# Five seven-product quads in each pass of the attention branch, with U summed ahead for four of them

## The chip, the cores and the metric

The kernel runs on one NeuronCore of a Trainium2 chip. The core has engines with queues of their own: TensorE (PE: matmuls and transposes, PEld: its weight loads), VectorE (DVE), ScalarE (ACT), GpSimd (POOL) and SyncE (SP, which issues most DMAs). Each engine works through its own list strictly in order, and waits where the next instruction needs something that another engine or a transfer has not yet delivered. The metric is the device time of one execution in microseconds.

## The reference

One layer of a hybrid block on 256 tokens of width 2048, in float32: a normed input is projected to q, k, v, gates and the inputs of a state-space part; attention with dilated windows over 16 heads and the state-space part each give a branch, which are merged through gates and projected once more.

```
hn = rms_norm(x, norm_w)
proj = hn @ w_in                                   # q, k, v, z_a, z_s, xbc, dt, g_a, g_s
...
o_a = o_a.reshape(b, s, ATTN_WIDTH) * jax.nn.silu(z_a)
...
merged = jax.nn.sigmoid(g_a) * (o_a @ w_attn_branch) + jax.nn.sigmoid(g_s) * (y @ w_ssm_branch)
return x + merged @ w_out
```

The change concerns the product `o_a @ w_attn_branch` (256 x 2048 by 2048 x 2048), called the attention branch below.

## The kernel before

**Splitting.** A float32 product is made of three matmuls on rounded parts: each factor is split into a high part h (a rounded copy) and a low part l (the rest), and `triple` adds xh·h, xh·l and xl·h. Weights come in units of 128 x 1024 (512 KB each), loaded by SyncE (L267) into a ring of five. For each unit ScalarE writes h (L278) and VectorE l = w - h (L279).

**Stages.** The units follow one another through the whole program: the state-space part until 744 us, v to 828, then 16 heads of q, k and za (828 to 1116), the gate ga (1116 to about 1200), the attention branch (about 1197 to 1284) and the output projection (to 1369). The last three, and v, go through `gemm_pair`.

**gemm_pair** makes 256 rows by 1024 columns in one pass, so that each stage has pass 0 (columns 0 to 1023) and pass 2 (1024 to 2047). It goes through eight quads; a quad is two rows of blocks of the weight (2 x 128 of the inner dimension). A plain quad takes two units and 24 matmuls of 128x512. A quad named in `S_QUADS` takes its 2 x 2 blocks by seven products (the Strassen-Winograd form), 21 matmuls. For it one needs sums of weights: A (wa, one whole unit, L530), C (wc, half a unit, L534), T (wt, 1024 wide, L533) and U = A's unit less T2, the right half of T. It also needs sums on the left, `sx_o`, made once for each quad from the heads' results (`keep_left`), kept in DRAM and fetched again (`fetch_left`, on POOL's queue). Each of A, C, T and U is split by ScalarE (L551) and VectorE (L552). The products that are shared go to four accumulators pp, the others straight to ps. `close`: the last quad of a pass, a plain one, finishes ps block by block.

**Sums ahead.** T of every such quad of ga, attn and out is made earlier: `sum_jobs` hangs, behind certain weight units of the heads, a load of two pieces (`get`), and three units later two subtracts and a transfer to DRAM (`add`, `spill`). There are 21 such jobs, one every 15/4 units. U is made in the branch itself: L565 on VectorE, between the splits of C and T.

**The end of a pass.** When all quads of seven products are in, `fold` (L589 to L594) adds the four accumulators pp together, L1154 adds ps, and `merge` (L1143, L1144) multiplies by the gate and adds the other branch: sixteen VectorE operations of 128x512, which give th_s. `turn_m` (L1136) transposes th_s on TensorE into banks "g", and `split` (L286, L288) writes mT, the left factor of the output projection. The accumulators pp of pass 2 lie in the same banks "g". `A_ORDERS` sets the order of the quads in each pass of the branch. The program's order decides the order on each engine, except where `high_priority` pulls a part forward (the splits of a quad, and the fold and merge of pass 2).

Of the kernel before, what the change touches and what calls it, by code (L numbers as in the profile page):

```python
# [15 lines left out]
P = 128  # L16
# [24 lines left out]
A_ORDERS = {0: (0, 1, 2, 4, 3, 6, 5, 7), 2: (0, 2, 1, 4, 3, 5, 6, 7)}  # L41
# [11 lines left out]
    ("attn", 0): (2, 4, 6), ("attn", 2): (2, 4, 5, 6), ("out", 0): (3, 5), ("out", 2): (3, 5),  # L53
# [6 lines left out]
O_BEHIND = 3, 14, 15, 17  # L60
SUMS_ATT = [(t, q) for t in [(n, c) for n in ("ga", "attn", "out") for c in (0, 2)] for q in S_QUADS[t]]
ATT_QUADS = sorted({*S_QUADS[("attn", 0)], *S_QUADS[("attn", 2)]})
# [136 lines left out]
def hybrid_block(ctx: ExitStack, tc: tile.TileContext, wall, xt, x, pk_d, cst_d, fw_d, out):  # L199
# [31 lines left out]
    presum, lefts = {}, {}  # L231
    ssm_pool = []

    def behind_unit(n, f):
        on_unit.setdefault(n, []).append(f)
# [8 lines left out]
    def sum_jobs(jobs, units, places):  # L244

        def get(tag, q, t, b11, behind):
            n = FIRST[tag] + 2 * q
            for dst, src in ((t, wall[n + 1]), (b11, wall[n, :, :512])):
                gp.tensor_copy(dst[:, 0:1], behind)
                nc.sync.dma_start(dst, src)  # L250

        def add(tag, q, t, b11, res, behind):
            gp.tensor_copy(res[:, 0:1], behind)
            ve.tensor_tensor(res[:, :512], t[:, :512], b11, ALU.subtract)
            ve.tensor_tensor(res[:, 512:], t[:, 512:], res[:, :512], ALU.subtract)
            spill(presum, (tag, q), f"t_{tag[0]}{tag[1]}_{q}", res, [UNIT])

        for n, ((tag, q), u) in enumerate(zip(jobs, units)):
            t, b11, res = places[n % len(places)]
            behind_unit(u, lambda behind, a=(tag, q, t, b11): get(*a, behind))  # L260
            behind_unit(u + SUM_LAG, lambda behind, a=(tag, q, t, b11, res): add(*a, behind))
# [207 lines left out]
    def gemm_pair(tag, x_of, n_kt, sxs, swap, extra={}, close=1, order=None, room={}, tail=None):  # L469
# [22 lines left out]
        for at, q in enumerate(order):  # L492
# [57 lines left out]
            def part(src, h, l):  # L550
                ac.activation(h, src, AF.Copy)  # L551
                ve.tensor_tensor(l, src, h.bitcast(F32), ALU.subtract)  # L552

            two = lambda t: t.rearrange("p (k m) -> p k m", k=2)
            with tc.high_priority(L_AHEAD):
# [8 lines left out]
                t2 = wt[:, 512:].unsqueeze(1).to_broadcast([P, 2, 512])  # L564
                ve.tensor_tensor(two(wa), two(wa), t2, ALU.subtract)  # L565
# [3 lines left out]
                part(wa, hu, lu)  # L569
# [122 lines left out]
    with tc.tile_pool(name="ssm", bufs=2) as sp:  # L692
# [212 lines left out]
        for c in GS_BEFORE[0]:  # L905
# [7 lines left out]
            [(sums_at[:, 0], sums_at[:, 2, :512], sums_at[:, 1])],  # L913
# [130 lines left out]
    with tc.tile_pool(name="att", bufs=2) as ap:  # L1044
# [33 lines left out]
        def mix(h, pT, za):  # L1078
# [10 lines left out]
            if h % 2 == 1 and q in ATT_QUADS:  # L1089
# [37 lines left out]
    with tc.tile_pool(name="fin", bufs=2) as fp:  # L1127
        fin = big.tile([P, 2, D], F32, name="fin", tag="yo1a")
        room = {"wt": [fin[:, i, UNIT:] for i in range(2)], "wc": [fin[:, i, :512] for i in range(2)]}
# [31 lines left out]
        attend(2)  # L1161
        for n in range(4):
            after(M_LAG + 1 + n // 2, lambda a=(2 + n // 2, n % 2, ("m1", "m2")[n % 2]): turn_m(*a))
# [119 lines left out]
```

## Time and profile before

| what | before |
|---|---|
| median of 3 runs | 1379.91 us (1379.5 to 1380.3) |
| the profiled execution | 1379.87 us, its span 1378.0 us |
| TensorE busy | 1366.8 us, granted clock 0.998 of full speed |
| VectorE busy | 1177.0 us |
| ScalarE busy | 840.0 us |
| heads, 828 to 1116 us | VectorE 218.31 of 288, DMA share 0.83 |
| attention branch, 1200 to 1284 us | TensorE 84.00, VectorE 75.21, DMA share 0.66 |

The span runs from the first to the last instruction that the profiler saw; the execution's own time has 1.87 us around it. Busy time of an engine is a sum over its instructions. In the lists of waits a row reads: engine and instruction that waited, what it waited for, then the total in us, how often, and the longest. In a timeline a row reads: start, length, engine, line, operation, output<-inputs, shapes, count.

### The profile page before, as it was taken

Reading aid. Unit: us, or ns where it says so; the run is one execution under the profiler, and the core shown is the slowest. Engines: PE = TensorE matmul, PEld = TensorE weight load, DVE = VectorE, ACT = ScalarE, POOL = GpSimd, SP = SyncE. Lnnn points to the kernel's source line nnn. Section 1 sums busy time; section 2 is a strip of 40 time slices with the busy share of each in tenths; the row PEclk is TensorE's granted clock in tenths of the full one; section 3 lists DMA queues with packets and bytes.
Section 4 is the critical chain, followed back from the end, with each engine's and each line's share of the span. In section 5 each row is a group of like instructions: output and inputs, shape, how many; then the busy total and the mean of one; then the engine's idle time right before and its main releaser. Section 6 shows DMA issues by size and latency. Waiting matters only on the chain.

```text
span 1378.0 us, 20734 instructions
## 1 busy us (share of the span) xinstructions
PE 1366.8 (99%) x7260; PEld 1164.8 (85%) x7260; DVE 1177.0 (85%) x1763; ACT 840.0 (61%) x1310; POOL 161.7 (12%) x238
## 2 busy tenths in 40 slices
PE   9999999999999999999999999999999999999997
PEld 7888888888888888888888888888888888888886
DVE  6898899898899888788989888777877789988897
ACT  7655777675667676666565554454444557655564
POOL 2301211101020100010001001211211000400112
PEclk9999999999999999999999999999999999999999
DMA  9767878778787867578677568888889757875773
GB/s 342 237 190 237 298 267 286 262 244 288 248 277 237 298 203 220 174 242 277 228 261 270 211 215 316 306 275 280 306 298 302 230 163 267 291 244 173 246 273 122
DMA packets 106520, 348.15 MB, mean 253 GB/s; under 512 B 11888, under 2 KB 14256, under 8 KB 106416
## 3 DMA queue, kind: packets, MB, share of 16 engines
q1 hardware_dynamic: 104400, 340.67, 74.0%
q10 hardware_dynamic: 1440, 4.06, 0.8%
q0 software_dynamic: 576, 2.10, 0.4%
q8 instruction: 57, 0.93, 0.3%
q14 instruction: 47, 0.39, 0.1%
HBM read 316.97 MB, written 29.82 MB: 252 GB/s over the span
## 4 chain that ended last, share of the span: by engine, by line
PE 98%; DMA 0%; DVE 0%; ACT 0%; issue 0%; SPq 0%; POOL 0%; POOLq 0%; DVEq 0%
PE ps_xs L333 8%; PE ps_zs L333 8%; PE ps_k L333 4%; PE ps_za L333 4%; PE ps_q L333 4%; PE ps_zs L339 4%; PE ps_xs L339 4%; PE ps_ssm L485 3%; PE ps_ssm L486 3%; PE ps_ssm L484 3%; PE ps_q L339 2%; PE ps_za L339 2%; PE ps_k L339 2%; PE ps_gs L421 2%; PE ps_gs L422 2%; PE ps_gs L420 2%
## 5 line engine op out<-in xcount | busy, mean ns | idle before, releaser
L278 ACT ACTIVATE h<-w 128x1024 fp32r<-128x1024 f32 (+1 forms) x394 | 410.0, 1048 | 306.0 <-issue 73.7
L279 DVE TENSOR_TENSOR l<-w,h 128x1024 fp32r<-128x1024 f32 (+1 forms) x394 | 474.0, 1209 | 111.1 <-ACT h L278 106.9
L333 PE MATMUL ps_zs<-XT,h 128*128 128x512 f32 x496 | 172.0, 393 | 0.0
L333 PE MATMUL ps_xs<-XT,h 128*128 128x512 f32 x496 | 171.6, 393 | 0.0
L339 PE MATMUL ps_zs<-XT,l 128*128 128x256 f32 x496 | 134.6, 279 | 0.0
L339 PE MATMUL ps_xs<-XT,l 128*128 128x256 f32 x496 | 133.7, 277 | 0.0
L333 PEld LDWEIGHTS ps_xs<-XT,h 128*128 128x128 f32 x496 | 91.3, 188 | 19.4
L333 PEld LDWEIGHTS ps_zs<-XT,h 128*128 128x128 f32 x496 | 91.3, 188 | 18.9
L339 PEld LDWEIGHTS ps_zs<-XT,l 128*128 128x128 f32 x496 | 93.3, 188 | 2.1
L339 PEld LDWEIGHTS ps_xs<-XT,l 128*128 128x128 f32 x496 | 93.2, 188 | 2.1
L333 PE MATMUL ps_q<-XT,h 128*128 128x512 f32 x256 | 91.1, 404 | 0.0
L333 PE MATMUL ps_k<-XT,h 128*128 128x512 f32 x256 | 88.6, 395 | 0.0
L333 PE MATMUL ps_za<-XT,h 128*128 128x512 f32 x256 | 88.4, 394 | 0.0
L551 ACT ACTIVATE ha<-wa 128x1024 fp32r<-128x1024 f32 x45 | 47.5, 1056 | 45.9 <-PE ps_ssm L486 10.0
L339 PE MATMUL ps_q<-XT,l 128*128 128x256 f32 x256 | 68.4, 278 | 0.0
L339 PE MATMUL ps_k<-XT,l 128*128 128x256 f32 x256 | 68.4, 277 | 0.0
L339 PE MATMUL ps_za<-XT,l 128*128 128x256 f32 x256 | 68.4, 277 | 0.0
L552 DVE TENSOR_TENSOR la<-wa,ha 128x1024 fp32r<-128x1024 f32 x45 | 54.8, 1218 | 8.4 <-ACT ha L551 8.3
L552 DVE TENSOR_TENSOR ltu<-wa,htu 128x1024 fp32r<-128x1024 f32 x40 | 48.7, 1219 | 10.8 <-ACT htu L551 10.8
L793 ACT ACTIVATE gt<-acb,acT 128x128 f32<-128x128 f32 x128 | 44.1, 390 | 22.2 <-DMA acb<-acum_d 21.9
L333 PEld LDWEIGHTS ps_k<-XT,h 128*128 128x128 f32 x256 | 47.0, 188 | 9.9
L333 PEld LDWEIGHTS ps_q<-XT,h 128*128 128x128 f32 x256 | 47.1, 188 | 9.7
(691 smaller groups left out, 3347.8 us busy)
## 6 DMA issues: line engine op xcount, KB each, us to landing
w<-in_wall SPq DMA_DIRECT2D x390, 512.0 KB, 4.8
wa<-in_wall SPq DMA_DIRECT2D x45, 512.0 KB, 4.7
th_a<-in_wall SPq DMA_DIRECT2D x21, 512.0 KB, 4.7
sums_at<-in_wall SPq DMA_DIRECT2D x18, 512.0 KB, 5.0
acb<-acum_d SPq DMA_DIRECT2D x32, 256.0 KB, 3.8
t_ssm<-sums_at SPq DMA_DIRECT2D x13, 512.0 KB, 4.3
wt<-t_ssm SPq DMA_DIRECT2D x13, 512.0 KB, 4.7
th_a<-in_wall SPq DMA_DIRECT2D x21, 256.0 KB, 5.4
```

Of the source, the lines that this page charges most:

```text
L278: ac.activation(h[:, a:b], w[:, a:b], AF.Copy)
L279: ve.tensor_tensor(l[:, a:b], w[:, a:b], h[:, a:b].bitcast(F32), ALU.subtract)
L333: high = pe.matmul(acc, h[:, kk, :], xs_of(kt), start=(kt == 0), stop=False)
L339: low = pe.matmul(acc[:, S:], l[:, kk, :], xs_of(kt)[:, :S], start=False, stop=(kt == KT - 1))
L420: pe.matmul(accs[i], xh, h[:, kk], start=(kt == 0), stop=False)
L421: pe.matmul(accs[i], xh, l[:, kk], start=False, stop=False)
L484: pe.matmul(acc, xh, h, start=start, stop=False)
L485: pe.matmul(acc, xh, l, start=False, stop=False)
L486: pe.matmul(acc, xl, h, start=False, stop=stop)
L551: ac.activation(h, src, AF.Copy)
L552: ve.tensor_tensor(l, src, h.bitcast(F32), ALU.subtract)
L793: ac.activation(g4[:, n, b], acb[:, j, b // 2 * P : b // 2 * P + P], AF.Relu, scale=-1.0, bias=sc[:, h : h + 1],)
```

## The change

In both passes of the branch the quads 2 to 6 use seven products (before: 2, 4, 6 in pass 0, and 2, 4, 5, 6 in pass 2), in the order 0, 2, 3, 1, 4, 5, 6, 7. For quads 3 to 6 U is summed ahead with T: the job then loads the whole second unit, makes one more subtract of 1024 and one more transfer to DRAM; the branch loads U (wu, L550 of the changed kernel) and leaves the subtract out. The 24 jobs come every 17/5 units. Their result lies in the pool of the converted units ("lt") and no longer in th_a. wu and wc lie in a pool of their own, `room_a`. A fifth left factor, for quad 3, is fetched together with the first.

```diff
-A_ORDERS = {0: (0, 1, 2, 4, 3, 6, 5, 7), 2: (0, 2, 1, 4, 3, 5, 6, 7)}
+A_ORDERS = {0: (0, 2, 3, 1, 4, 5, 6, 7), 2: (0, 2, 3, 1, 4, 5, 6, 7)}
...
-    ("attn", 0): (2, 4, 6), ("attn", 2): (2, 4, 5, 6), ("out", 0): (3, 5), ("out", 2): (3, 5),
+    ("attn", 0): (2, 3, 4, 5, 6), ("attn", 2): (2, 3, 4, 5, 6), ("out", 0): (3, 5), ("out", 2): (3, 5),
...
-O_BEHIND = 3, 14, 15, 17
+U_QUADS = 3, 4, 5, 6
+O_BEHIND = 3, 3, 14, 15, 17
...
+SUMS_U = {(t, q) for t, q in SUMS_ATT if t[0] == "attn" and q in U_QUADS}
...
-        def get(tag, q, t, b11, behind):
+        def get(tag, q, t, b, behind):
             n = FIRST[tag] + 2 * q
-            for dst, src in ((t, wall[n + 1]), (b11, wall[n, :, :512])):
+            b = b if (tag, q) in SUMS_U else b[:, :512]
+            for dst, src in ((t, wall[n + 1]), (b, wall[n, :, : b.shape[-1]])):
                 gp.tensor_copy(dst[:, 0:1], behind)
                 nc.sync.dma_start(dst, src)
 
-        def add(tag, q, t, b11, res, behind):
+        def add(tag, q, t, b, res, behind):
+            res = res(f"t_{tag[0]}{tag[1]}_{q}")
             gp.tensor_copy(res[:, 0:1], behind)
-            ve.tensor_tensor(res[:, :512], t[:, :512], b11, ALU.subtract)
+            ve.tensor_tensor(res[:, :512], t[:, :512], b[:, :512], ALU.subtract)
             ve.tensor_tensor(res[:, 512:], t[:, 512:], res[:, :512], ALU.subtract)
             spill(presum, (tag, q), f"t_{tag[0]}{tag[1]}_{q}", res, [UNIT])
+            if (tag, q) in SUMS_U:
+                t2 = res[:, 512:].unsqueeze(1).to_broadcast([P, 2, 512])
+                two = b.rearrange("p (k m) -> p k m", k=2)
+                ve.tensor_tensor(two, two, t2, ALU.subtract)
+                spill(u_sums, (tag, q), f"u_{tag[0]}{tag[1]}_{q}", b, [UNIT])
...
+            if (tag, q) in u_sums:
+                wu = place("wu")
+                nc.sync.dma_start(wu, u_sums[tag, q])
...
-                t2 = wt[:, 512:].unsqueeze(1).to_broadcast([P, 2, 512])
-                ve.tensor_tensor(two(wa), two(wa), t2, ALU.subtract)
+                if (tag, q) not in u_sums:
+                    wu = wa
+                    t2 = wt[:, 512:].unsqueeze(1).to_broadcast([P, 2, 512])
+                    ve.tensor_tensor(two(wa), two(wa), t2, ALU.subtract)
                 ht, lt = pair_of("t")
                 part(wt, ht, lt)
                 hu, lu = pair_of("u")
-                part(wa, hu, lu)
+                part(wu, hu, lu)
...
-            SUMS_ATT, [FIRST[("q", 0)] + 3 + n * 15 // 4 for n in range(len(SUMS_ATT))],
-            [
-                (th_a[:, i, :UNIT], th_a[:, 1, UNIT + 512 * i : UNIT + 512 * i + 512], th_a[:, 0, UNIT:])
-                for i in range(2)
-            ],
+            SUMS_ATT, [FIRST[("q", 0)] + 3 + n * 17 // 5 for n in range(len(SUMS_ATT))],
+            [(th_a[:, i, :UNIT], th_a[:, i, UNIT:]) for i in range(2)],
+            lambda name: mul.tile([P, UNIT], F32, name=name, tag="lt", bufs=2),
...
-    with tc.tile_pool(name="fin", bufs=2) as fp:
+    with tc.tile_pool(name="branch", bufs=1) as bp:
         fin = big.tile([P, 2, D], F32, name="fin", tag="yo1a")
-        room = {"wt": [fin[:, i, UNIT:] for i in range(2)], "wc": [fin[:, i, :512] for i in range(2)]}
+        spots = bp.tile([P, 3 * UNIT], F32, name="room_a", tag="room_a")
+        room = {
+            "wt": [fin[:, i, UNIT:] for i in range(2)],
+            "wu": [spots[:, i * UNIT : (i + 1) * UNIT] for i in range(2)],
+            "wc": [spots[:, 2 * UNIT + i * 512 : 2 * UNIT + i * 512 + 512] for i in range(2)],
+        }
```

What stands where on the engines, at three places of the program. In the names, `attn0` and `attn2` are the passes; the first number after h, l, ha, la, hc, lc, htt, ltt, htu, ltu is the weight unit (pass 0 has 417 to 432, pass 2 has 433 to 448, two for each quad, so that 429 is quad 6 of pass 0 and 437 quad 2 of pass 2), and the last number only tells buffers apart.

VectorE, from the first fold operation of pass 0 on (the sum of pp_attn0_2). Before:

```order
L591 TENSOR_TENSOR fin_12298<-pp_attn0_2_12380,fin_12298 128x512
L279 TENSOR_TENSOR l432_12589<-w432_12586,h432_12588 128x1024
L552 TENSOR_TENSOR ltt437_12721<-fin_12298,htt437_12720 128x1024
L592 TENSOR_TENSOR fin_12298<-pp_attn0_3_12381,fin_12298 128x512
L593 TENSOR_TENSOR fin_12298<-fin_12298 128x512
L279 TENSOR_TENSOR l433_12670<-w433_12667,h433_12669 128x1024
L594 TENSOR_TENSOR fin_12298<-fin_12298 128x512
L279 TENSOR_TENSOR l434_12676<-w434_12673,h434_12675 128x1024
L1154 TENSOR_TENSOR fin_12298<-ps_attn0_0_12299,fin_12298 128x512
L1154 TENSOR_TENSOR fin_12298<-ps_attn0_1_12300,fin_12298 128x512
L1143 SCALAR_TENSOR_TENSOR th_a_7802<-th_a_7802,fin_12298 128x512 x2
L1154 TENSOR_TENSOR fin_12298<-ps_attn0_2_12301,fin_12298 128x512
```

And in the changed kernel:

```order
L605 TENSOR_TENSOR fin_12386<-pp_attn0_2_12433,fin_12386 128x512
L606 TENSOR_TENSOR fin_12386<-pp_attn0_3_12434,fin_12386 128x512
L1171 TENSOR_TENSOR fin_12386<-ps_attn0_0_12388,fin_12386 128x512
L564 TENSOR_TENSOR ltt437_12822<-fin_12386,htt437_12821 128x1024
L607 TENSOR_TENSOR fin_12386<-fin_12386 128x512
L1160 SCALAR_TENSOR_TENSOR th_a_7802<-th_a_7802,fin_12386 128x512
L564 TENSOR_TENSOR la437_12813<-wa437_12808,ha437_12812 128x1024
L564 TENSOR_TENSOR lc437_12817<-room_a_12387,hc437_12816 128x512
L608 TENSOR_TENSOR fin_12386<-fin_12386 128x512
L1171 TENSOR_TENSOR fin_12386<-ps_attn0_1_12389,fin_12386 128x512
L1161 SCALAR_TENSOR_TENSOR th_s_90<-th_a_7802,th_s_90 128x512
L579 TENSOR_TENSOR wa437_12808<-wa437_12808,fin_12386 128x1024
```

What moved: the splits of quad 7 (l432) and of the first quad of pass 2 (l433, l434) stood among the fold, and now stand ahead of it; the splits of quad 2 of pass 2 (la437, lc437, U437) stand among it instead. The list goes on with:

```order
L564 TENSOR_TENSOR la439_12856<-wa439_12850,ha439_12855 128x1024
L1171 TENSOR_TENSOR fin_12386<-ps_attn0_2_12390,fin_12386 128x512
L1171 TENSOR_TENSOR fin_12386<-ps_attn0_3_12391,fin_12386 128x512
L564 TENSOR_TENSOR lc439_12860<-room_a_12387,hc439_12859 128x512
L1160 SCALAR_TENSOR_TENSOR th_a_7802<-th_a_7802,fin_12386 128x512
L288 TENSOR_TENSOR l435_12895<-w435_12892,h435_12894 128x1024
L564 TENSOR_TENSOR ltu437_12826<-wa437_12808,htu437_12825 128x1024
L1160 SCALAR_TENSOR_TENSOR th_a_7802<-th_a_7802,fin_12386 128x512 x2
L1161 SCALAR_TENSOR_TENSOR th_s_90<-th_a_7802,th_s_90 128x512
L288 TENSOR_TENSOR l436_12901<-w436_12898,h436_12900 128x1024
```

TensorE, from the last matmul on pp_attn0_2 on. Before:

```order
L486 MATMUL pp_attn0_2_12380<-htt429_12515,sx_o6_12315 128x512
L484 MATMUL ps_attn0_0_12299<-h427_12546,oaTb_10585 128x512
L484 MATMUL ps_attn0_1_12300<-h427_12546,oaTb_10585 128x512
L484 MATMUL ps_attn0_3_12302<-h427_12546,oaTb_10585 128x512
L484 MATMUL pp_attn0_3_12381<-htu429_12519,sx_o6_12315 128x512
L484 MATMUL ps_attn0_2_12301<-htu429_12519,oaTb_10585 128x512
L485 MATMUL ps_attn0_0_12299<-l427_12547,oaTb_10585 128x512
L486 MATMUL ps_attn0_0_12299<-h427_12546,oaTb_10585 128x512
L485 MATMUL ps_attn0_1_12300<-l427_12547,oaTb_10585 128x512
```

And in the changed kernel:

```order
L495 MATMUL pp_attn0_2_12433<-htt429_12652,sx_o6_12404 128x512
L494 MATMUL pp_attn0_3_12434<-ltu429_12657,sx_o6_12404 128x512
L495 MATMUL pp_attn0_3_12434<-htu429_12656,sx_o6_12404 128x512
L494 MATMUL ps_attn0_2_12390<-ltu429_12657,oaTb_10649 128x512
L495 MATMUL ps_attn0_2_12390<-htu429_12656,oaTb_10649 128x512
L493 MATMUL ps_attn0_2_12390<-h431_12683,oaTb_10649 128x512
L494 MATMUL ps_attn0_2_12390<-l431_12684,oaTb_10649 128x512
L495 MATMUL ps_attn0_2_12390<-h431_12683,oaTb_10649 128x512
L493 MATMUL ps_attn0_2_12390<-h432_12689,oaTb_10649 128x512
```

What moved: before, quad 5 (unit 427) and quad 7 stood behind the last products of quad 6; now only quad 7 does, whose first blocks (ps_attn0_0, 1 and 3) stand even ahead of them. Further on TensorE begins the quads of pass 2 and the transposes; before, around the first l of quad 1 (435):

```order
L1136 MATMUL mtp10_12653<-cst_77,th_s_90 128x128 x3
L1136 MATMUL mtp11_12660<-cst_77,th_s_90 128x128 x3
L485 MATMUL ps_attn2_1_12636<-lc437_12716,sx_o2_12082 128x512
L486 MATMUL ps_attn2_1_12636<-hc437_12715,sx_o2_12082 128x512
L484 MATMUL ps_attn2_1_12636<-h435_12751,oaTa_8484 128x512
L484 MATMUL ps_attn2_2_12637<-htu437_12724,oaTa_8484 128x512
L485 MATMUL ps_attn2_0_12635<-l435_12752,oaTa_8484 128x512
L486 MATMUL ps_attn2_0_12635<-h435_12751,oaTa_8484 128x512
```

and in the changed kernel from the place where la of quad 3 is used:

```order
L494 MATMUL ps_attn2_0_12736<-la439_12856,oaTa_8484 128x512
L495 MATMUL ps_attn2_0_12736<-ha439_12855,oaTa_8484 128x512
L493 MATMUL ps_attn2_0_12736<-h435_12894,oaTa_8484 128x512
L494 MATMUL ps_attn2_1_12737<-lc439_12860,sx_o3_12170 128x512
L495 MATMUL ps_attn2_1_12737<-hc439_12859,sx_o3_12170 128x512
L493 MATMUL ps_attn2_1_12737<-h435_12894,oaTa_8484 128x512
L494 MATMUL ps_attn2_0_12736<-l435_12895,oaTa_8484 128x512
```

What moved: quad 3 (439) with its la and lc has come in between quad 2 and quad 1, and twelve of the sixteen transposes stand behind quad 1 now. From the last matmul on pp_attn0_2 to the first on pp_attn2_0 stood 112 matmuls and 16 transposes before, and 61 and 16 in the changed kernel.

More of the change, by code (lines that the diff above doesn't have):

```diff
@@ L230, in hybrid_block @@
     on_unit = {}
-    presum, lefts = {}, {}
+    presum, u_sums, lefts = {}, {}, {}
     ssm_pool = []
@@ L912, in hybrid_block @@
             SUMS_SSM, [FIRST[("B", g)] + n for g in range(1, 7) for n in SUM_UNITS],
-            [(sums_at[:, 0], sums_at[:, 2, :512], sums_at[:, 1])],
+            [(sums_at[:, 0], sums_at[:, 2, :512])], lambda name: sums_at[:, 1],
         )
@@ L1161, in hybrid_block @@
         attend(2)
+    with tc.tile_pool(name="fin", bufs=2) as fp:
         for n in range(4):
```

8 lines of the change are left out of this document (4 added, 4 removed).

## The prediction

> **What bounds the kernel now.** I read the page from the chain of work backwards, and asked first whether the engine that the chain names ever stops.
>
> ```profile
> span 1378.0 us, 20734 instructions
> PE 1366.8 (99%) x7260; PEld 1164.8 (85%) x7260; DVE 1177.0 (85%) x1763; ACT 840.0 (61%) x1310; POOL 161.7 (12%) x238
> PE 98%; DMA 0%; DVE 0%; ACT 0%; issue 0%; SPq 0%; POOL 0%; POOLq 0%; DVEq 0%
> PE warm L630 <- DVE ssq L627: 1.4, 1, 1.4
> PE ps_first L385 <- ACT h L278: 1.4, 2, 1.1
> ```
>
> 98% of the chain is TensorE, and the two last rows are the whole answer of the view of waits for that engine: three waits, 2.8 us, in 1378 us. So the kernel is as long as its row of matmuls, and two things alone change the time: fewer matmuls, or a wait that TensorE does not have today. The price of a matmul is read where the attention branch runs:
>
> ```profile
> 1226.52 0.39 PE L484 MATMUL ps_attn<-hc,sx_o 128*128 128x512 f32 x1
> ...
> 1227.88 0.39 PE L485 MATMUL pp_attn<-ltt,sx_o 128*128 128x512 f32 x1
> ```
>
> The first column is the start. Six steps take 1.36 us: 0.227 us for each matmul, though each row lasts 0.39 (they overlap).
>
> **What goes.** A plain quad issues 24 matmuls, one with seven products 21. The branch goes from seven such quads (three, then four) to ten: 9 matmuls fewer, 9 x 0.227 = **-2.04 us**. That is all that the change can gain, since TensorE waits for nothing that could go away.
>
> **What is added in the heads (828 to 1116 us).** Three more sums (21 to 24), and eight of them now also make U.
>
> ```profile
> 828.00:1116.00 288.00, 288.00 (x1684) 253.15 (x1683) 218.31 (x417) 142.25 (x220) 43.57 (x63) 1.00 0.83 281
> L254 DVE TENSOR_TENSOR th_a<-th_a x21: 681/691/693, 836.1 to 1063.6; 128x512 f32<-128x512 f32 x21
> L565 DVE TENSOR_TENSOR wa<-wa,fin x7: 1214/1217/1218, 1208.1 to 1273.7; 128x1024 f32<-128x1024 f32 x7
> ACT h L278 <- PE ps_za L333: 31.8, 20, 1.8
> ACT h L278 <- PE ps_k L333: 18.7, 11, 1.8
> ACT h L278 <- PE ps_q L333: 13.6, 11, 1.6
> ```
>
> The columns of the first row are the length, then the busy time of PE, PEld, DVE, ACT and POOL, the granted clock, the DMA share and GB/s. VectorE has 288 - 218 = 70 us free. It gets 6 subtracts of 0.69, 8 of 1.22 and one more left factor (six small operations, estimated at 2.5 us from the 0.69 of a row 512 wide): some 16 us. The last three rows show who leads: ScalarE's conversions wait for TensorE to give buffers back (its list of waits here has no row that ends on a weight load). So the conversions run ahead, and the added subtracts take from that lead: **0 us**. If the cover were gone, each would cost at most its own 1.2 us.
>
> The loads are nearer their limit. Over seven heads (126 us, at 288 / 16 = 18 each) the order of SyncE's queue now has 45.4 MB where it had 37.2 (86.5 pieces of 512 KB, not 71: three sums more, U's other half loaded, U spilled). The row's 281 GB/s at a share of 0.83 would be 338 at a share of 1, and 45.4 MB at 338 are 134 us: 8 us late over these heads if 338 were the limit. But more has been moved elsewhere:
>
> ```profile
> 1196.00:1202.00 6.00, 6.00 (x28) 4.99 (x27) 4.65 (x7) 2.80 (x4) 0.99 (x3) 1.00 1.00 382
> ```
>
> At 382 GB/s they take 119 us, inside 126. I take 0, being nearer to a rate that was measured at full share than to a scaled one, and keep 8 us as the other end. [...]
>
> The new loads of U (512 KB each, in place of nothing) fall into 1160 to 1284:
>
> ```profile
> 1160.00:1200.00 40.00, 39.98 (x178) 32.80 (x176) 37.94 (x41) 27.73 (x34) 14.72 (x8) 1.00 0.83 283
> 1200.00:1242.00 42.00, 42.00 (x187) 34.79 (x186) 37.91 (x43) 24.84 (x29) 0.00 (x0) 1.00 0.74 250
> 1242.00:1284.00 42.00, 42.00 (x195) 34.83 (x194) 37.30 (x45) 24.07 (x31) 3.16 (x1) 1.00 0.58 184
> ```
>
> Shares of 0.83, 0.74 and 0.58 leave room for eight of them (4 MB, 11 us at 382 GB/s, beside 84 us of the branch). The two first stand in SyncE's queue ahead of the load of wa407; its first use moves some 24 matmuls (5.4 us) later in TensorE's order, more than the 2.7 us that two such loads take. **0 us.** Inside the passes a further quad of seven costs VectorE 1.5 conversions more, and U ahead saves it a subtract; counted along the order, VectorE's lead grows in pass 0 and stays above 2 us at the step to the last product.
>
> **The hand-over from pass 0 to pass 2 is what decides.** VectorE ran here in before, in the order that the change touches:
>
> ```profile
> 1229.90 0.68 DVE L591 TENSOR_TENSOR fin<-pp_attn,fin 128x512 f32<-128x512 f32 x1
> ...
> 1237.57 1.28 DVE L1154 TENSOR_TENSOR fin<-ps_attn,fin 128x512 f32<-128x512 f32 x2
> 1238.77 1.28 DVE L1143 SCALAR_TENSOR_TENSOR th_a<-th_a,fin 128x512 f32<-128x512 f32 x2
> ...
> 1247.65 2.35 DVE L279 TENSOR_TENSOR l<-w,h 128x1024 fp32r<-128x1024 f32 x2
> 1249.92 1.22 DVE L552 TENSOR_TENSOR ltu<-wa,htu 128x1024 fp32r<-128x1024 f32 x1
> 1251.06 2.47 DVE L288 TENSOR_TENSOR mT<-mtp,mT 128x512 fp32r<-128x512 f32 x4
> 1249.04 2.04 ACT L286 ACTIVATE mT<-mtp 128x512 fp32r<-128x512 f32 x4
> 1247.16 0.82 PE L1136 MATMUL mtp<-cst,th_s 128*128 128x128 f32 x6
> 1247.73 0.48 PE L484 MATMUL ps_attn<-hc,sx_o 128*128 128x512 f32 x1
> 1255.57 0.39 PE L484 MATMUL pp_attn<-ha,oaTa 128*128 128x512 f32 x1
> ```
>
> From start to start an operation 512 wide costs 1.20 / 2 = 0.60 us (1237.57 to 1238.77), one of 1024 costs 2.27 / 2 = 1.135 us (1247.65 to 1249.92), and a transpose 0.57 / 6 = 0.095 us of TensorE (1247.16 to 1247.73). The fold can begin only when the last product of pp_attn0_2 is in. Then sixteen operations of 512 (fold, add, merge) lead to th_s, its transposes, mT, and only then does pp_attn2_0 get the banks that the transposes used. In before, TensorE had 112 matmuls and 16 transposes between that last product and the first of pp_attn2_0 (25.4 + 1.5 = 26.9 us; the trace has 1228.1 to 1255.57). The sixth place in the order held the last quad of seven, with two plain quads behind it. In the new order it is the seventh with one behind it, and the rows of order leave **61 matmuls and 16 transposes**: 13.8 + 1.5, with about 0.3 for switching, 15.6 us.
>
> VectorE's list from L605 on is the sixteen, and mixed into them the conversions that pass 2 starts with. Up to l436 stand 16 operations of 512 and 7 of 1024 (ltt437, la437, U437, la439, l435, ltu437, l436): 16 x 0.60 + 7 x 1.135 + 0.3 for start and end = 17.85 us after the last product. TensorE would like l436 after 55 matmuls and 4 transposes: 12.9 us. It comes 4.95 us late; la439 (made at 10.2, wanted at 8.8), lc439 (12.0, 9.5) and l435 (13.8, 10.2) are late before it, as parts of the same wait. From l436 on stand six matmuls (1.4), twelve transposes (1.1), and ScalarE's copy and VectorE's split of the first part of mT (0.51 and 0.62, quarters of the rows of four). pp_attn2_0 would start at 20.4 if the two lay wholly beside the later transposes, at 21.5 if none of it did; I take 21.15, since only part of the transposes is left once the first bank is full. That is 21.15 instead of 15.6: **+5.55 us**.
>
> How sure is the count? The same count for before gives every tile there at least 0.7 us of lead, and TensorE indeed does not wait. Where both can be compared, the count can be kind:
>
> ```profile
> 1242.97 1.22 DVE L552 TENSOR_TENSOR la<-wa,ha 128x1024 fp32r<-128x1024 f32 x1
> ...
> 1246.61 0.48 PE L485 MATMUL ps_attn<-la,oaTa 128*128 128x512 f32 x1
> ```
>
> la437 was ready at 1244.19 and used at 1246.61, a lead of 2.4 us where the count has 4.6. So the wait is bounded by 4.1 us below (VectorE's list as far as mT alone, 19.7, against 15.6) and by 7 above (most of those 2.2 us more). I take 5.55, which the rows give as they stand.
>
> **The sum,** made against the profiled run: 1379.87 (span 1378.0 and 1.87 around it; the median is 1379.91, so they are one): 1379.87 - 2.04 + 5.55 = **1383.4 us**.
>
> **The rivals.** *The hand-over is covered*: TensorE keeps running, only the nine matmuls count: 1379.87 - 2.04 = 1377.8, on the faster side. For it speaks that TensorE waits nowhere in before, though VectorE is as full there (37.9 of 42 us). It decides where VectorE reaches l436 in 12.9 us instead of 17.85, which needs each operation at 72% of the measured price, or five of the sixteen and two conversions gone from ahead of it. Against it stands that the list is a fixed order. 0.19.
> *The loads of the heads bind*: at 338 GB/s seven heads are 8 us late, of which a ring of loads hides some; with the hand-over 1388 to 1392. For it: VectorE and SyncE issue in order, and a share of 0.83 is high. Against: 382 was reached, and before shows no wait for a load. 0.09.
> *Half the wait*: if the sums and merges that stand ahead of la439 and l435 found gaps to run in, some 2.8 us of wait would remain: 1380.6. VectorE's list has no gap there by the count, so this stays thin: 0.02.
>
> **How the numbers follow.** The forecast has 0.70, from 1382.0 to 1385.0 by its bounds of 4.1 and 7 (1381.9 and 1384.8, rounded). To leave out no more than 2 in 10 the range goes down to the covered hand-over: 1377.6 to 1385.4; what it leaves out is mostly the loads. A difference under 0.2% (2.76 us: 1377.1 to 1382.6) is about what a measurement of this kernel can't tell from no change. The lower end of the forecast lies inside that, so of its 0.70 I count 0.14 as the same and 0.56 as slower; the loads add 0.02 and 0.07. The covered hand-over is the same but for 0.03 (2.04 us are not 2.76), 0.16, and half the wait adds 0.02: faster 0.03, same 0.34, slower 0.63.
>
> **What would show it.** In the trace of after, right: 354 matmuls in the branch; TensorE's list of waits has rows on la, lc and l of L564 and L288 for VectorE between the two passes, some 4 to 7 us, and the granted clock stays at 1.00. Wrong: no such row and the end near 1377.8; or waits between 828 and 1116 us for h or l behind a weight load; or an order of the merge that leaves more than 61 matmuls ahead of pp_attn2_0.

## The result, and the profile after

| | before | changed kernel |
|---|---|---|
| median | 1380.30 us (5 runs, 1379.5 to 1381.0) | 1389.19 us (5 runs, 1388.2 to 1391.4) |
| ratio | 1 | 1.0067, interval 1.0054 to 1.0079 |
| the profiled execution | 1379.87 us, span 1378.0 | 1388.82 us, span 1387.0 |

The change costs 8.9 us, where 3.5 were forecast. Each ratio, here and below, is to runs of the kernel before that were taken beside it; their medians lie between 1380.3 and 1381.0 us, so that differences to before can be compared between experiments more safely than times. The page of the changed kernel, its span, busy times and the chain that ended last, and then the view of waits for TensorE, without its four rows of 0.2 and 0.3 us (instruction that waited, what for, total in us, times, longest):

```profile
span 1387.0 us, 20876 instructions
PE 1370.0 (99%) x7251; PEld 1164.8 (84%) x7251; DVE 1190.0 (86%) x1784; ACT 845.2 (61%) x1317; POOL 168.7 (12%) x249
PE 95%; DVE 2%; DMA 1%; issue 1%; ACT 1%; POOL 0%; SPq 0%; POOLq 0%; ACTq 0%; DVEq 0%
PE ps_out L495 <- DVE mT L297: 2.0, 1, 2.0
PE ps_attn L494 <- DVE l L288: 1.5, 2, 0.8
PE warm L644 <- DVE ssq L641: 1.4, 1, 1.4
PE ps_attn L493 <- ACT htu L563: 0.9, 1, 0.9
PE ps_first L394 <- ACT h L287: 0.8, 1, 0.8
PE ps_attn L494 <- DVE lc L564: 0.6, 1, 0.6
PE pp_attn L493 <- DVE mT L297: 0.4, 1, 0.4
PE ps_attn L493 <- ACT h L287: 0.4, 1, 0.4
...
```

Two rows of waits have become twelve, and the chain has 95% of TensorE instead of 98%. TensorE has 9 matmuls fewer (7251 for 7260) and is yet busy for 3.2 us more: some of what is lost counts as busy time, so the rows of waits do not hold it all. I went along the starts of TensorE's matmuls instead, and added up by how much each step from start to start is longer than the usual 0.227 us (0.095 for a transpose). From the gate to the end this gives four places:

| place | lost, us |
|---|---|
| gate (1149) | 0.45 |
| first hand-over, pass 0 to pass 2 (1247 to 1260.3) | 5.80 |
| end of pass 2 (1283 to 1285) | 1.02 |
| second hand-over, branch to output projection (1308 to 1314) | 3.86 |
| 9 matmuls less | -2.04 |
| sum | 9.09 (the spans differ by 9.0) |

By the same count the kernel before loses about 0.3 us at the first hand-over and 0.2 at the second, so that the sum comes within 0.1 us of the spans partly by luck.

**The first hand-over** went as the count along the lists had it. VectorE's and TensorE's timeline of the changed kernel (start, length, engine, line, operation):

```profile
1238.94 0.69 DVE L605 TENSOR_TENSOR fin<-pp_attn,fin 128x512 f32<-128x512 f32 x1 [4.21 <-PE pp_attn L495]
...
1255.57 1.21 DVE L288 TENSOR_TENSOR l<-w,h 128x1024 fp32r<-128x1024 f32 x1
...
1238.52 0.39 PE L495 MATMUL pp_attn<-htt,sx_o 128*128 128x512 f32 x1
...
1256.84 0.50 PE L494 MATMUL ps_attn<-l,oaTa 128*128 128x512 f32 x1 [0.69 <-DVE l L288]
...
1260.25 0.50 PE L493 MATMUL pp_attn<-ha,oaTa 128*128 128x512 f32 x1 [0.43 <-DVE mT L297]
```

From the end of the step of the last product (1238.52 + 0.23 = 1238.75) l436 is ready after 18.0 us (1255.57 + 1.21 = 1256.78; counted 17.85), and pp_attn2_0 starts after 21.5 (counted 21.15). VectorE had stood idle for 4.2 us ahead of L605: it waits there for the last product, and nothing that stands behind L605 in its list ran in that time. The tiles that TensorE waited for were, in this order, h435 and htu437 from ScalarE, and lc439, l435, l436 and mT from VectorE (and for 0.2 us th_s, for a transpose). The prediction had named those four; its la439 was ready by the time that ScalarE's two tiles let TensorE go on, and these it had not counted. The waits in the rows add up to 4.0 us. The rest of the 5.80 counts as busy: a row lasts 0.39 us where the next start would follow after 0.227, and behind each wait a step takes some 0.1 us more.

**The second hand-over** was priced at nothing. VectorE, ScalarE, TensorE, and the window behind the wait (length; busy time of PE, PEld, DVE, ACT, POOL; granted clock; DMA share; GB/s):

```profile
1305.33 1.22 DVE L564 TENSOR_TENSOR la<-wa,ha 128x1024 fp32r<-128x1024 f32 x1
1308.90 1.23 DVE L579 TENSOR_TENSOR wa<-wa,room_o 128x1024 f32<-128x1024 f32 x1 [2.36 <-DMA room_o<-t_out]
1310.04 1.28 DVE L297 TENSOR_TENSOR mT<-mtp,mT 128x512 fp32r<-128x512 f32 x2
...
1306.00 1.09 ACT L295 ACTIVATE mT<-mtp 128x512 fp32r<-128x512 f32 x2 [2.21 <-PE mtp L1153]
...
1308.40 0.39 PE L494 MATMUL ps_out<-l,mT 128*128 128x512 f32 x1
1310.78 2.08 PE L495 MATMUL ps_out<-h,mT 128*128 128x512 f32 x4 [2.00 <-DVE mT L297]
1312.65 0.63 PE L493 MATMUL ps_out<-h,mT 128*128 128x512 f32 x1
1313.08 0.63 PE L494 MATMUL ps_out<-l,mT 128*128 128x512 f32 x1
...
1310.70:1314.20 3.50, 3.42 (x8) 2.77 (x9) 3.50 (x7) 2.68 (x4) 0.14 (x1) 0.51 0.63 213
```

L579 is U455, the sum U of the first seven-product quad of the output projection (quad 3, units 455 and 456). It needs T455, whose load lands at 1308.9. That load starts late for a reason that the view of waits for SyncE's queue names, first in the changed kernel and then in before:

```profile
SPq L542 <- DVE th_s L1161: 0.9, 1, 0.9
SPq L533 <- DVE th_s L1144: 0.9, 1, 0.9
```

T455 lies in `room_o`, which takes the place of th_a (both have the tag "yo1b" in the kernel), and the last operation of `merge` still reads th_a. So the load is issued only at 1304.3, as that operation ends, 1 us before TensorE begins the last transposes for mT (1305.3). In VectorE's list it stands ahead of all four splits of mT, so mT, whose first two parts ScalarE had copied by 1307.1, waits for a load that it does not need. TensorE stands for 2.16 us, and the eight matmuls behind it run at a granted clock of 0.51, 0.427 us from start to start: 1.7 us more. In before, the first split of mT stood ahead of U455, and U455 waited 1.87 us without harm:

```profile
1301.21 0.69 DVE L288 TENSOR_TENSOR mT<-mtp,mT 128x512 fp32r<-128x512 f32 x1 [0.66 <-ACT mT L286]
1303.77 1.22 DVE L565 TENSOR_TENSOR wa<-wa,room_o 128x1024 f32<-128x1024 f32 x1 [1.87 <-DMA room_o<-t_out]
```

**The end of pass 2**, on ScalarE and TensorE of the changed kernel:

```profile
1282.80 1.06 ACT L563 ACTIVATE htt<-fin 128x1024 fp32r<-128x1024 f32 x1 [4.06 <-PE pp_attn L495]
...
1283.92 0.73 PE L493 MATMUL pp_attn<-htt,sx_o 128*128 128x512 f32 x2 [0.24 <-ACT htt L563]
1284.86 0.51 PE L493 MATMUL pp_attn<-htu,sx_o 128*128 128x512 f32 x1 [0.22 <-ACT htu L563]
```

ScalarE waits for TensorE to be done with the last quad's T before it may convert the next (in the kernel the converted T and U share two buffers), and then TensorE waits for ScalarE.

**The heads** held:

```profile
828.00:1116.00 288.00, 288.00 (x1684) 253.22 (x1683) 231.16 (x437) 143.12 (x221) 51.44 (x72) 1.00 0.90 318
```

VectorE has 12.9 us more (16 estimated), the DMA engines 318 GB/s instead of 281 at a share of 0.90, and TensorE is busy for the whole 288 us.

### The profile page after: what moved, and what is told of

Same layout as the page of the kernel before. It is cut to its first block, busy times and chain, and to the rows that moved or that the text cites. A ratio compares the mean times of both kernels' runs of the same rounds, so it can differ in the third digit from the quotient of the medians.

```text
span 1387.0 us, 20876 instructions
## 1 busy us (share of the span) xinstructions
PE 1370.0 (99%) x7251; PEld 1164.8 (84%) x7251; DVE 1190.0 (86%) x1784; ACT 845.2 (61%) x1317; POOL 168.7 (12%) x249
## 4 chain that ended last, share of the span: by engine, by line
PE 95%; DVE 2%; DMA 1%; issue 1%; ACT 1%; POOL 0%; SPq 0%; POOLq 0%; ACTq 0%; DVEq 0%
PE ps_xs L342 8%; PE ps_zs L342 8%; PE ps_za L342 4%; PE ps_k L342 4%; PE ps_q L342 4%; PE ps_zs L348 4%; PE ps_xs L348 4%; PE ps_ssm L494 3%; PE ps_ssm L495 3%; PE ps_ssm L493 3%; PE ps_q L348 2%; PE ps_za L348 2%; PE ps_k L348 2%; PE ps_gs L430 2%; PE ps_gs L431 2%; PE ps_gs L429 2%
## 5 line engine op out<-in xcount | busy, mean ns | idle before, releaser
L287 ACT ACTIVATE h<-w 128x1024 fp32r<-128x1024 f32 (+1 forms) x388 | 403.5, 1047 | 303.5 <-issue 66.9
L288 DVE TENSOR_TENSOR l<-w,h 128x1024 fp32r<-128x1024 f32 (+1 forms) x388 | 466.6, 1209 | 104.4 <-ACT h L287 98.9
L563 ACT ACTIVATE ha<-wa 128x1024 fp32r<-128x1024 f32 x48 | 50.7, 1056 | 43.9 <-PE ps_ssm L495 10.2
L564 DVE TENSOR_TENSOR la<-wa,ha 128x1024 fp32r<-128x1024 f32 x48 | 58.5, 1219 | 7.8 <-ACT ha L563 7.7
L342 PEld LDWEIGHTS ps_za<-XT,h 128*128 128x128 f32 x256 | 46.9, 188 | 9.8
```

Of the source, the lines that this page charges most:

```text
L287: ac.activation(h[:, a:b], w[:, a:b], AF.Copy)
L288: ve.tensor_tensor(l[:, a:b], w[:, a:b], h[:, a:b].bitcast(F32), ALU.subtract)
L342: high = pe.matmul(acc, h[:, kk, :], xs_of(kt), start=(kt == 0), stop=False)
```

## The experiments

Two theories. **Order**: the loss is waits at the hand-overs, set by what stands ahead of what in the lists of VectorE and ScalarE. **Bytes**: the loss is the added traffic and the added sums. Edits are to the changed kernel unless said otherwise.

**e1: T455 through another queue.**

```diff
-                nc.sync.dma_start(wt, presum[tag, q])
+                (nc.gpsimd if (tag, q) == (("out", 0), 3) else nc.sync).dma_start(wt, presum[tag, q])
```

> The changed kernel, with one load moved: T of unit 455 (the first seven-product quad of the output projection) goes through POOL's queue and no longer stands in SyncE's behind the load of wa455. Theory (order at the second hand-over): in the changed kernel TensorE stood 2.0 us before the last third of the products with mT, because VectorE had U455 ahead of all four splits of mT in its list and U455 waited 2.4 us for T455; after it eight matmuls took 0.427 us each instead of 0.227 (1.6 us). With T455 there early, and with mT ahead of U455 in VectorE's list, both go: 1389.2 - 3.8 = 1385.4 us, no window with a granted clock of 0.5 near 1311 us. Rival (bytes): the loss is the added traffic; the same bytes move, so it stays at 1389 and the wait comes back elsewhere.

Measured: 1392.28 us, ratio 1.0083 (1.0069 to 1.0097): slower still, a miss. TensorE's largest wait and ScalarE's timeline:

```profile
PE ps_out L493 <- ACT mT L295: 4.9, 1, 4.9
1311.78 0.63 ACT L563 ACTIVATE hc<-room_o 128x512 fp32r<-128x512 f32 x1 [6.87 <-DMA room_o<-in_wall]
1312.31 2.04 ACT L295 ACTIVATE mT<-mtp 128x512 fp32r<-128x512 f32 x4
```

VectorE's list now had mT ahead of U455, but ScalarE's had hc455, which waits for another load (C455), ahead of its four copies of mT. The same thing on another engine: ScalarE stood for 6.9 us before an operation that waits for a load, with mT's copies behind it. That speaks for order, though not as I had expected it. T455 did not come earlier either: POOL issued it at 1305.7, after the last `merge` operation, for which it waited like SyncE before; C455 lies in `room_o` too and was issued at 1305.5.

**e2: x through another queue.** The four loads of x that ScalarE issues go to POOL's queue.

```diff
-                lambda behind, i=i, cs=cs: fetch(fin[:, i, cs], x[i * P : (i + 1) * P, cs], behind, nc.scalar),
+                lambda behind, i=i, cs=cs: fetch(fin[:, i, cs], x[i * P : (i + 1) * P, cs], behind, nc.gpsimd),
```

> The changed kernel, with the four loads of x for the end issued from POOL's queue and not ScalarE's. In the changed kernel POOL's small copy ahead of the second of them lasted 4.6 us and ScalarE stood 5.2 us before it; then came the conversion whose l frees the ring place for wa455, and T455 stands behind wa455. Theory A (the held ScalarE made T455 late): T455 lands some 3 us earlier, U455 does not wait, TensorE's 2.0 us wait and the 1.6 us at half clock go: about 1385.5. Theory B (SyncE's queue is late for another reason, the ring itself): the load of T455 stays where it is relative to TensorE, and the time at 1389.

Measured: 1388.09 us, ratio 1.0050 (1.0036 to 1.0064). ScalarE's 5.2 us ahead of h are gone, and SyncE's queue and VectorE look as before:

```profile
1304.17 0.33 SPq L542 DMA_DIRECT2D room_o<-t_out  x1
1310.19 1.23 DVE L579 TENSOR_TENSOR wa<-wa,room_o 128x1024 f32<-128x1024 f32 x1 [3.59 <-DMA room_o<-t_out]
PE ps_out L495 <- DVE mT L297: 1.7, 1, 1.7
```

The load of T455 is issued at 1304.2 (1304.3 in the changed kernel), and U455 waits for it even longer. Theory A falls: the time at which ScalarE was held did not make the load late. As in the changed kernel the load is issued when the last `merge` operation ends (1304.1). The time is lower than the changed kernel's, but the intervals of the two ratios overlap, so that no gain is shown. In this profile the first hand-over lost 1.0 us more than in the changed kernel and the second 1.8 us less: the four matmuls behind the wait took 1.20 us there, for 2.08. The mean granted clock of this profile is 0.995 (0.997 in the changed kernel).

**e3: the old quads.** Old `S_QUADS` and `A_ORDERS` of the branch, old `O_BEHIND`, old spacing of 15/4; U ahead stays for five quads, and so do the pools.

> The changed kernel with the old set of seven-product quads, the old orders of the branch, the old pace of the sums and the old four left factors: what stays of the change is U summed ahead for the five of its quads that are in U_QUADS (its loads, its subtracts in the heads, its spills), the pools and the buffers. Theory (order at the hand-overs): 114 matmuls stand between the last product on pp_attn0_2 and the first on pp_attn2_0, so no wait there; the heads cover the sums: 1379.5 to 1381. Rival (bytes and VectorE's added sums in the heads, or the U loads in the branch): most of the loss stays, in proportion five eighths of it: 1385.

Measured: 1381.90 us, ratio 1.0009 (1.0000 to 1.0018). In TensorE's list of waits one row is left, the one at the start (`warm`). U ahead for five quads, its loads and its pools cost about 1 us of the 8.9 (0 to 2.5 by the interval), which can hardly be told from nothing. Bytes as the main cause falls for the branch and the heads: five of the eight sums of U are still made, spilled and loaded.

**e4: other orders of the same work.**

```diff
-A_ORDERS = {0: (0, 2, 3, 1, 4, 5, 6, 7), 2: (0, 2, 3, 1, 4, 5, 6, 7)}
+A_ORDERS = {0: (0, 2, 3, 4, 5, 1, 6, 7), 2: (0, 1, 2, 3, 4, 5, 6, 7)}
```

> The changed kernel with other orders of the quads in the branch: pass 0 has plain quad 1 in the sixth place (0, 2, 3, 4, 5, 1, 6, 7), pass 2 starts with both plain quads (0, 1, 2, 3, 4, 5, 6, 7). Same matmuls, same bytes, same VectorE work. Theory (order): 77 matmuls instead of 61 between the last product on pp_attn0_2 and the first on pp_attn2_0, and the splits that pass 2 starts with are those of plain quads; counted along the lists the worst tile is 1.4 us late instead of 4.9, so the wait at the first hand-over falls from 5.8 to 1.5 to 2.5 us: 1385 to 1386, the second hand-over unchanged. Rival (bytes, VectorE's sum of work): 1389 as before, with four seven-product quads in a row perhaps more.

Measured: 1389.60 us, ratio 1.0063 (1.0050 to 1.0076). The time is a miss. The first hand-over went as expected: 0.5 us of waits are left, of 4 in the rows of the changed kernel, and by the steps 2.1 us for 5.8. What was won there came back behind it, where the second hand-over had been expected unchanged (the profiled run, 1391.83 us, is the slowest of the five):

```profile
PE ps_out L495 <- DVE mT L297: 3.0, 1, 3.0
PE pp_attn L493 <- ACT htt L563: 1.7, 2, 1.4
PE pp_attn L493 <- ACT htu L563: 0.7, 2, 0.5
PE ps_attn L494 <- DVE la L564: 0.3, 1, 0.3
PE ps_attn L493 <- ACT hc L563: 0.2, 1, 0.2
1312.30:1318.20 5.90, 5.81 (x14) 4.56 (x15) 5.90 (x11) 2.68 (x4) 0.18 (x1) 0.50 0.54 195
```

With five seven-product quads one behind the other in pass 2 (three in the changed kernel) the two buffers of T and U cost 2.4 us of waits instead of 0.4, and 5.3 us by the steps, for 1.0. The mean granted clock of this profile is 0.995 (0.997 in the changed kernel). At the second hand-over TensorE waits for mT for 3.0 us and then runs 14 matmuls at a granted clock of 0.50 (3 us).

**e5: U455 behind mT.** U455 is multiplied by a factor of 1 that is made from mT, so that it cannot stand ahead of it; loads and queues stay.

```diff
-                    ve.tensor_tensor(two(wa), two(wa), t2, ALU.subtract)
+                    if (tag, q) == (("out", 0), 3):
+                        one = behind_mt["out"]
+                        ve.tensor_scalar(one, x_of(8)[:, S : S + 1].bitcast(F32), 0.0, 1.0, ALU.mult, ALU.add)
+                        ve.scalar_tensor_tensor(two(wa), two(wa), one, t2, ALU.mult, ALU.subtract)
+                    else:
+                        ve.tensor_tensor(two(wa), two(wa), t2, ALU.subtract)
```

> The changed kernel, with U of unit 455 (output projection) made to depend on the first split part of mT, by a factor of 1 that is computed from it: VectorE's list now has the first two splits of mT ahead of U455, and the loads stay as they are. Theory (order: one VectorE operation that waits for T455 stands ahead of mT): the 2.0 us wait at the second hand-over goes, though T455 lands where it did, and the half clock behind it: 1389.2 - 3.8 = 1385.4 us. What is left of mT (two parts behind U455) is wanted late enough. Rival (T455's landing is what counts, wherever U stands): the wait only moves to the next user, ltt455 or mT, and the time stays within 1 us of 1389.

Measured: 1387.57 us, ratio 1.0050 (1.0036 to 1.0064). VectorE and TensorE:

```profile
1307.94 1.29 DVE L297 TENSOR_TENSOR mT<-mtp,mT 128x512 fp32r<-128x512 f32 x2
...
1310.46 1.28 DVE L583 SCALAR_TENSOR_TENSOR wa<-wa,one,room_o 128x1024 f32<-128x1024 f32 x1 [0.50 <-DMA room_o<-t_out]
...
1309.72 0.39 PE L495 MATMUL ps_out<-l,mT 128*128 128x512 f32 x1
1309.94 1.07 PE L496 MATMUL ps_out<-h,mT 128*128 128x512 f32 x4
```

U455 still waits for its load, but two parts of mT are split ahead of it, and TensorE goes from the second products to the third without a break. The whole wait at the second hand-over is gone, and the half clock with it: the matmuls from 1310.85 to 1311.98 start 0.23 us apart. From TensorE's first matmul of ga to its last of the program the two profiles differ by 3.5 us; the medians differ by 1.6 only. The profile of e5 lost 1.4 us ahead of ga, where the edit does not reach, 1.1 of it at the very start (`ps_first`, whose waits lie between 0 and 1.9 us in the twelve profiles). The ratio is the same as that of e2, and its interval overlaps that of the changed kernel. So it is the trace that shows the repair, and the medians alone would not. (The lines of this kernel are shifted by one to six.)

**e6: four and five.** Quads 2, 3, 4, 6 in pass 0, both passes in the old orders.

> The changed kernel with the quads 2, 3, 4, 6 of seven products in pass 0, and both passes in their old orders: (0, 1, 2, 4, 3, 6, 5, 7) with two plain quads behind the last of seven products, and (0, 2, 1, 4, 3, 5, 6, 7). 9 such quads, 6 matmuls fewer than before (-1.4 us). 88 matmuls stand between the last product on pp_attn0_2 and the first on pp_attn2_0 (61 in the changed kernel, 112 before). Theory (order at the hand-overs): by the count the worst tile is 0.8 us late, so a wait of 0.8 to 2.5 us there; VectorE's list has all of mT ahead of U455, so none at the second hand-over: 1380.5 to 1382.5. Rival (bytes, sums): nine of the ten sums move, so 1387 to 1388.

Measured: 1382.14 us, ratio 1.0008 (0.9999 to 1.0017): within the forecast, and no gain over before. In the branch one wait of TensorE is left (0.5 us, for an l). Six matmuls fewer are 1.4 us, and they do not show in the time: by the steps the first hand-over loses 1.2 us more than in before, and a late ha at the end of ga 0.4.

**e7: the order alone, on the kernel before.**

```diff
-A_ORDERS = {0: (0, 1, 2, 4, 3, 6, 5, 7), 2: (0, 2, 1, 4, 3, 5, 6, 7)}
+A_ORDERS = {0: (0, 1, 2, 4, 3, 5, 6, 7), 2: (0, 2, 1, 4, 3, 5, 6, 7)}
```

> The kernel before, with one edit: quads 5 and 6 change places in pass 0, so that the last quad of seven products is the seventh, as in the changed kernel. Nothing is added. Theory in its simple form (the place of the last such quad sets the wait): 67 matmuls instead of 112 before pp_attn2_0, a wait of 4 to 6 us: 1385 or 1386. Theory in its full form (place and what VectorE's list has to do there): pass 2 begins with quads 0, 2, 1, of which only one is of seven products, and by the count along the list every tile keeps 0.4 us; mT is then the only thing late: 0 to 2.5 us: 1380.5 to 1383. In this order U455 also stands ahead of mT in VectorE's list, so the second hand-over may lose up to 4 us here as well, without any added load; if it does, the list and not the bytes is what loses them.

Measured: 1387.00 us, ratio 1.0046 (1.0034 to 1.0059). Two numbers changed places, nothing was added, and 6 us are lost. TensorE's largest waits, and VectorE's U455 at the second hand-over:

```profile
PE ps_out L486 <- DVE mT L288: 2.0, 1, 2.0
PE ps_attn L484 <- ACT htu L551: 0.8, 1, 0.8
PE ps_attn L484 <- ACT hc L551: 0.4, 1, 0.4
...
1306.74 1.23 DVE L565 TENSOR_TENSOR wa<-wa,room_o 128x1024 f32<-128x1024 f32 x1 [2.49 <-DMA room_o<-t_out]
```

By the steps of TensorE 3.2 us go at the first hand-over and 2.2 at the second. (The profiled run is the fastest of the five, 1385.05 us.) The second is lost as in the changed kernel, mT's first split following U455 at 1307.9, without one byte or one sum more: the list loses it. The first loses little more than half of what it does in the changed kernel. Pass 2 begins with fewer splits here, and six matmuls more stand ahead of pp_attn2_0; which of the two counts was not separated.

**e8: U not ahead.** `U_QUADS = ()`.

> The changed kernel without U summed ahead (U_QUADS empty): ten quads of seven products, U by VectorE in the branch, no loads, spills and subtracts for U in the heads. Theory (order at the hand-overs): 65 matmuls at the first one, the worst tile 5.2 us late by the count: wait 5 to 6.5; U455 ahead of mT, so 2 to 4 at the second; VectorE has 8 subtracts of 1.2 more in the branch, which have 10 us of idle time in all to go into: 1389 to 1392. Rival (bytes): 8.4 MB fewer in the heads and the branch, so most of the loss goes: 1381 to 1384.

Measured: 1395.77 us, ratio 1.0108 (1.0094 to 1.0122): 15 us above its before, for 8.9 in the changed kernel, beyond both forecasts and far from the rival's. Both hand-overs wait. For the further losses the rows name other causes than VectorE's eight subtracts. At the end of ga (3.0 us of waits) ScalarE stands for loads of wa and w, and at the end of pass 2 (2.5 us on one htt) behind POOL:

```profile
1289.17 1.06 ACT L564 ACTIVATE htt<-fin 128x1024 fp32r<-128x1024 f32 x1 [3.72 <-POOL fin L660]
```

There ScalarE has to issue a load of x, which waits for a one-column copy on POOL (last section). With U ahead ten quads of seven products are about 6 us faster in this program; how much of that is the subtracts themselves was not separated. Its price is the 1 us or so of e3.

**e9: both hand-overs eased.** e5, with `A_ORDERS = {0: (0, 2, 3, 4, 5, 1, 6, 7), 2: (0, 2, 1, 3, 4, 5, 6, 7)}`.

> The changed kernel with both hand-overs eased: pass 0 in the order (0, 2, 3, 4, 5, 1, 6, 7), pass 2 in (0, 2, 1, 3, 4, 5, 6, 7), and U455 behind the first two splits of mT as in e5. All ten quads of seven products, all loads and sums as in the changed kernel. Theory (the loss is the sum of waits set by the order of the lists): 76 matmuls at the first hand-over, the worst tile 2.4 us late by the count, so 2.4 to 3.5 there; none at the second; some 1 us late in pass 2, where three quads in a row wait for the two buffers of T and U; 0.9 for what stayed in e3: 1380.7 - 2.0 + 3.0 + 1.0 + 0.9 = 1383.6, range 1382.5 to 1386 (the upper end if the clock halves behind the waits). Rival (bytes): 1387 or more.

Measured: 1384.11 us, ratio 1.0026 (1.0016 to 1.0036), 0.5 us from the sum of waits. By the steps 3.2 us are lost at the first hand-over (3.0 expected), 2.1 at the end of pass 2 (1.0 expected) and nothing at the second hand-over. TensorE's waits in the branch:

```profile
PE ps_attn L494 <- ACT htu L564: 1.2, 1, 1.2
PE ps_attn L495 <- DVE ltu L565: 0.8, 1, 0.8
PE pp_attn L494 <- ACT htu L564: 0.5, 2, 0.3
PE pp_attn L494 <- ACT htt L564: 0.5, 2, 0.3
```

All ten quads, all bytes and all sums are there, and 5 of the 8.9 us are back, by two orders and one dependence. Bytes as the main cause falls.

**e10: four and four.** Quads 2, 3, 4, 6 and 2, 4, 5, 6, old orders.

> The changed kernel with eight quads of seven products (2, 3, 4, 6 in pass 0; 2, 4, 5, 6 in pass 2) in the old orders: one such quad more than before, 3 matmuls fewer (-0.7 us). 88 matmuls at the first hand-over, mT20 ahead of U455 at the second, only one splits' list as full as in e6. Theory (order): a wait of 0.5 to 1.5 us at the first hand-over, none at the second, so within 1 us of e6 and of before: 1380.5 to 1382.2. Rival (each such quad costs by its bytes): 1381.9.

Measured: 1383.35 us, ratio 1.0022 (1.0013 to 1.0031), above the range by 1.1 us. The first hand-over loses as much as in e6 (1.6 us by the steps). But at the second, U455 stands behind the first split of mT, as expected, and waits much longer than the 0.9 us of e6:

```profile
1307.93 1.23 DVE L579 TENSOR_TENSOR wa<-wa,room_o 128x1024 f32<-128x1024 f32 x1 [4.29 <-DMA room_o<-t_out]
```

So ltt455, lc455 and ltu455, which stand behind U455 in VectorE's list, come late, and TensorE loses 1.3 us at them (1310 to 1315). Another 0.5 us go at 1282, where an operation of ScalarE (`fin`) is late; e6 has neither loss. No version was faster than the kernel before.

## Why the prediction was wrong

- **What bounds the kernel** was right: TensorE's row of matmuls and its waits give the time. The 9 matmuls are gone as counted (2.04 us).
- **The first hand-over** was right in mechanism and size: 5.55 forecast, 5.80 measured (l436 ready after 18.0 us for 17.85), though two of the tiles waited for on the way were ScalarE's. The two allowances of 0.3 us in the forecast, for switching and for start and end, were my estimates and stand in no row; for before, the count of steps without such an allowance came to 26.9 us from the last product to pp_attn2_0, where the trace has 27.5 (1228.11 to 1255.57). e4 took most of it away by order alone, e9 nearly half.
- **The heads** at nothing held, and so did the loads: 318 GB/s, no wait. e3 puts what U ahead costs for five quads at about 1 us, with 2.5 as the end of its interval.
- **The step that failed** is the sentence that VectorE's lead "stays above 2 us at the step to the last product", and the 0 us for the loads beside it. It counted VectorE's list as if every operation could start once the one ahead was done. U455 cannot: it waits for the load of T455, 2.4 us in the changed kernel and 1.9 us in before, where the row was to be seen and did no harm. What matters in VectorE's two lists there is whether U455 stands ahead of mT or behind its first part, and I had not compared them there. e7 makes this wait without adding anything, e5 removes it with everything else in place. Measured: 2.16 us of standing and 1.7 us of half clock, 3.86 us for the 0 of the prediction, which had also expected the granted clock to stay at 1.00.
- **The end of pass 2** was in the same 0: 1.0 us, because three seven-product quads in a row leave ScalarE no free buffer for T and U. e4, with five in a row, makes it 2.4 us of waits; the buffers themselves were not varied, so that part is read from the waits only. The gate's 0.45 us stays unexplained; e7, whose edit comes only later in the program, loses about half as much at the same place.
- **The rivals**: covered and half the wait did not happen. The time of the third, the loads of the heads (1388 to 1392 us), holds the measured one, but by chance: its mechanism did not happen, since TensorE waits for nothing in the heads. None of the three had a wait at the second hand-over. The range's upper end held the first hand-over at its worst and nothing beside it.

What stays open: the gate's 0.45 us, why the loads at the end of ga are late in e8, and how much of the spread of the changed kernel's runs (1388.2 to 1391.4) is half clock. The mean clocks of these five runs go from 0.998 (the fastest run) to 0.995, and the 3.4 us at half clock behind the second hand-over of the profiled run lower its mean by 0.0012, so that 0.003 is what two or three such stretches would make; but the slowest run has 0.996 and not the lowest clock.

## What to carry to other kernels

Where engines work through fixed lists, compare the lists at every hand-over and ask of each operation what it waits for, loads included: one that waits for a load costs nearly its whole wait ahead of the tile that the bounding engine wants next (2.16 us of TensorE's standing for a wait of 2.36 us in the changed kernel), and behind it only what outlasts the lead of the tiles that follow (nothing for a wait of 1.9 us in before, 1.3 us for one of 4.3 us in e10). Ask also what the load itself waits for: here its place in memory came free only 1 us before the transposes of the wanted tile began. A change of order far upstream can turn one into the other, so an edit that only moves a quad (e7) can cost more than the work that the change adds. And saving a few per cent of a stage's matmuls brought nothing here (e6), where the end of the stage is a chain on another engine; leave the work that covers that chain behind it.

## What the runs showed of the hardware

- The granted clock fell behind some short waits of TensorE's and not behind others. In the changed kernel it was 0.51 from 1310.7 to 1314.2, after TensorE had stood 2.16 us, and two matmuls started 0.43 us apart there (1312.65 to 1313.08) where the usual step is 0.227; the first hand-over, 5.8 us lost in waits of at most 1.2 us each, left it at 1.00 (1247 to 1260). In e1 the rows of waits on htu, lc and h at the first hand-over are the same as in the changed kernel (0.9, 0.6 and 0.4 us), and the granted clock was 0.50 from 1251.3 to 1257.4. In e4 it was 0.50 from 1312.3 to 1318.2, behind a wait of 3.0 us. In e7 a wait of 2.1 us left no half clock behind it: the next matmuls start 0.23 us apart (1309.66 to 1309.89). So the length of a wait alone does not tell these runs apart, and what does was not shown.
- POOL's one-column copy ahead of a load took 4.6 us in the changed kernel, ending (1300.27) as VectorE's unbroken row of operations ended (1300.21), and ScalarE, which had to issue that load, stood for 5.2 us. Another such copy (2.9 us) ended at 1281.74 there, as a row of VectorE's ended (1281.69). Taking ScalarE out of it (e2) did not change the time by more than the runs differ; in e8 the same hold of ScalarE (3.72 us) made a tile late, and TensorE waited 2.5 us for it. Whether VectorE's row held the copy was not tested.
